# Two-layer hybrid trunk on one core: elementwise work of GpSimd moved to VectorE, norm sums and gate results in pieces, six raw buffers

## Chip, core and metric

The kernel runs on one core of a Trainium2 chip. The metric is the device time of one execution in microseconds (us). A profiled execution gives a trace: every instruction of TensorE (PE, its weight loads PEld), VectorE (DVE), ScalarE (ACT), GpSimd (POOL) and the DMA queue of SyncE (SP), with its start, its duration and what it waited for.

## What is computed

Batch 1, 256 tokens, width 2048, two layers, all in float32. Layer 0 has a Mamba-2 mixer (SSD), layer 1 forgetting attention (FoX). Cut to the frame:

```python
for i in range(DEPTH):
    hn = rmsnorm(h, norm_mix_pre[i])
    mix = ssd_mixer(hn, ...) if i % 2 == 0 else fox_mixer(hn, ...)
    h = h + rmsnorm(mix, norm_mix_post[i])
    ff = swiglu(rmsnorm(h, norm_ffn_pre[i]), ffn_w_gate[i], ffn_w_up[i], ffn_w_down[i])
    h = h + rmsnorm(ff, norm_ffn_post[i])
    pe = rmsnorm(p[i] @ ple_w_proj[i], ple_norm[i])
    h = h + jax.nn.sigmoid(h @ ple_w_gate[i]) * pe
```

rmsnorm divides by the root of the mean square over the 2048 features and multiplies by a weight. The last line of a layer is the per-layer input (PLE below).

## The kernel before

**Tiles.** h is kept transposed as 16 chunks `h[c]` of 128 features x 256 tokens. All weights (515 MB) stream from HBM once. A matmul input is split in two parts that together hold the float32: for activations `x[:, 0]` and `x[:, 1]` (`split`), for weights `wh` (a cast on ScalarE, L174) and `wl` (raw - wh on VectorE, L176). Each pair of weight tile and chunk gives TensorE a matmul of 512 columns (wh, L233) and one of 256 (wl, L235).

**Stages and units.** A unit is a product for 2 to 6 tiles of 128 outputs over all K chunks. It is cut into stages of at most 1024 weight columns: one chunk for a six-tile unit, two for a four-tile one, four for the two-tile one. A stage loads `raw` over SyncE's queue, casts wh and subtracts wl; raw, wh and wl have four buffers each. `next_stage` issues a stage two ahead (LOOK). After a unit the sums of its accumulators leave PSUM through `gather` (a copy on ScalarE, an add on VectorE). Six accumulator banks are shared by the units.

**Background.** `bg` is a list of small tasks; `unit` takes one after each stage. `drain` runs what is left. A scheduler with a timeline model of its own then orders the instructions of each engine; `tc.issue_after` holds an instruction behind another.

**An update.** After the mixer and after the FFN, `post_norm` forms 1/rms of the result (sums of squares in `ssb`, a matmul with ones, a power on GpSimd L287, a diagonal `dg` and one more matmul into `rwide`). The first unit that follows carries `mk_update`: for chunk c it adds the normed part `ts[c]` to h (L422 on VectorE; from c = 3 on every second chunk on GpSimd, L424), forms the next `ts` (L414), splits h into the next unit's input (L265 with a weight, L262 without), and, ahead of the FFN, squares h on ScalarE and adds the square to `ssb` on GpSimd (L274). Update A stands in the first gate unit of the FFN, update B in the first gate unit of PLE; there is one of each in each layer. The six-tile unit needs one chunk each stage.

**The FFN's first gate unit** also has `mk_r` at its end, which turns `ssb` into `rwide` and half of it, `rwide2`; then `ev_g` gathers each tile and forms silu (L487, a tanh on ScalarE, L490, L491), with the sums of squares of `pp` (`ssp`) as background of the up unit.

**PLE.** `pp` is p @ W_proj, `ssp` its sum of squares; `mkpe` forms `rpe`, `mkpp` scales pp on GpSimd (L537). Four units of 6, 4, 4 and 2 tiles compute the gate. `e3` closes a tile at the unit's end: tanh on ScalarE, L555 (tanh + 1 times pp), L556 (times weight, added to h), in layer 0 also the split for the attention (L265 into xb) and the square with its sum on GpSimd; in layer 1 it stores the chunk.

**V.** The attention of layer 1 starts with five units for V, with tokens as output rows: matmuls of 412 columns, wl of 824, eight stages each. At the end of the first stands the 1/rms of h.

**Start.** `prep0` splits each chunk of x as it arrives and adds its square to `ssb` on GpSimd; the first unit has five tiles and one chunk a stage.

## Time and profile before

| | before |
|---|---|
| median of 3 runs | 2798.67 us (2798.58 to 2799.8) |
| profiled execution | 2800.33 us |
| its span (first to last instruction) | 2798.5 us |
| TensorE's clock as granted, mean | 0.999 |

The busy time of an engine is the sum of its instructions; of two that overlap in the engine's pipeline the overlap counts once. A row of the timeline gives start and duration, engine, source line, operation, output<-inputs and the shape, and in brackets the idle time before it and what ended it. In a table of windows the columns are the window, its length, busy time and instructions of each engine asked for (TensorE alone, or TensorE, its weight loads, VectorE, ScalarE, GpSimd), then the granted clock as a share of full speed, the share of the DMA engines' time and GB/s. A row of waits gives what waited, for what, us in total, how often, and the longest.

### The profile page before, as it was taken

What the parts mean: (1) busy time and instruction counts of PE and PEld (TensorE: products, weight loads), DVE (VectorE), ACT (ScalarE), POOL (GpSimd) and SP (SyncE); (2) the same over time, 40 slices, a digit from 0 to 9 for tenths busy, and PEclk for the clock granted to TensorE, in tenths of its full rate; (3) what the DMA queues carried; (4) which work ended last, traced back from release to release, by engine and by line L of the source; (5) the groups of instructions that cost most, each with busy time, mean ns of one, the idle gap of its engine ahead of it and who ended that gap; (6) DMA issues with size and microseconds to landing.
All of it is one profiled execution on the core that took longest, in us unless ns stands there. A gap on an engine that the chain in (4) does not pass through costs nothing.

```text
span 2798.5 us, 43191 instructions
## 1 busy us (share of the span) xinstructions
PE 2768.2 (99%) x16306; PEld 2447.5 (87%) x16306; DVE 1926.0 (69%) x3033; ACT 1484.8 (53%) x2455; POOL 183.5 (7%) x236
## 2 busy tenths in 40 slices
PE   9999999999999999999999999999999999999999
PEld 8888888889788888888897998888888888888888
DVE  8888888855966645666669656766866545666577
ACT  6587676644654444444446544555654444445454
POOL 2000000000300000000005000000200000000022
PEclk9999999999999999999999999999999999999999
DMA  7666665565566656666555676655666556656545
GB/s 235 189 197 183 194 191 177 158 202 180 161 201 189 192 191 188 188 180 194 194 168 167 189 207 191 178 161 166 181 189 192 192 190 187 195 172 204 192 153 176
DMA packets 262512, 520.09 MB, mean 186 GB/s; under 512 B 17392, under 2 KB 42128, under 8 KB 262304
## 3 DMA queue, kind: packets, MB, share of 16 engines
q1 hardware_dynamic: 258640, 504.96, 58.8%
q0 software_dynamic: 3520, 12.15, 1.5%
q8 instruction: 127, 2.08, 0.3%
q14 instruction: 81, 0.66, 0.1%
q10 hardware_dynamic: 144, 0.24, 0.0%
HBM read 515.10 MB, written 2.18 MB: 185 GB/s over the span
## 4 chain that ended last, share of the span: by engine, by line
PE 91%; DVE 4%; issue 4%; ACT 1%; POOL 0%; DMA 0%; DVEq 0%; ACTq 0%; POOLq 0%
PE acc L233 53%; PE acc L235 28%; PE acc L230 1%; PE acc L229 1%; PE acc L228 1%; PE acc L223 1%; PE acc L222 1%; PE acc L224 1%; PE mi L751 1%; DVE x L265 1%; DVE wl L176 1%; DVE sg L414 1%; DVE x L262 0%; DVE h L422 0%; PE mi L753 0%
## 5 line engine op out<-in xcount | busy, mean ns | idle before, releaser
L233 PE MATMUL acc<-x,wh 128*128 128x512 f32 x5008 | 1718.9, 394 | 13.7 <-DVE x L265 6.6
L176 DVE TENSOR_TENSOR wl<-raw,wh 128x1024 fp32r<-128x1024 f32 (+4 forms) x1020 | 1183.2, 1166 | 782.4 <-ACT wh L174 778.8
L174 ACT CAST wh<-raw 128x1024 fp32r<-128x1024 f32 (+4 forms) x1020 | 1006.6, 993 | 989.0 <-PE acc L233 809.9
L235 PE MATMUL acc<-x,wl 128*128 128x256 f32 x5008 | 1340.0, 283 | 7.5 <-DVE wl L176 7.5
L233 PEld LDWEIGHTS acc<-x,wh 128*128 128x128 f32 x5008 | 928.2, 188 | 209.5 <-DVE x L265 14.7
L235 PEld LDWEIGHTS acc<-x,wl 128*128 128x128 f32 x5008 | 932.5, 189 | 33.1 <-DVE wl L176 10.9
L233 PE MATMUL acc<-a,wh 128*128 128x512 f32 x1232 | 425.5, 391 | 0.0
L235 PE MATMUL acc<-a,wl 128*128 128x256 f32 x1232 | 341.9, 282 | 0.0
L233 PEld LDWEIGHTS acc<-a,wh 128*128 128x128 f32 x1232 | 229.9, 188 | 47.1
L235 PEld LDWEIGHTS acc<-a,wl 128*128 128x128 f32 x1232 | 232.6, 189 | 2.2
L233 PE MATMUL acc<-xb,wh 128*128 128x512 f32 x512 | 181.9, 396 | 0.0
L256 ACT COPY tb<-acc 128x256 f32<-128x256 f32 (+1 forms) x401 | 139.6, 369 | 38.6 <-PE acc L235 19.0
L235 PE MATMUL acc<-xb,wl 128*128 128x256 f32 x512 | 145.8, 285 | 0.0
L287 POOL TENSOR_TENSOR rs<-ms,mhalf 128x2 f32<-128x2 f32 x18 | 21.2, 1177 | 1752.8 <-DVE ms L284 1752.8
L233 PEld LDWEIGHTS acc<-xb,wh 128*128 128x128 f32 x512 | 95.9, 188 | 19.3
L235 PEld LDWEIGHTS acc<-xb,wl 128*128 128x128 f32 x512 | 96.7, 189 | 0.7 <-issue 0.2
L257 DVE TENSOR_TENSOR g<-acc,tb 128x256 f32<-128x256 f32 x204 | 78.7, 415 | 2.1 <-ACT tb L256 1.6
L233 PE MATMUL acc<-xq,wh 128*128 128x512 f32 x224 | 77.6, 390 | 0.0
L733 ACT ACTIVATE E<-ab,bias 128x128 f32<-128x128 f32 x192 | 59.8, 390 | 15.3 <-PE mi L753 14.7
L661 DVE SCALAR_TENSOR_TENSOR g<-xr,vec,g 128x256 f32<-128x256 f32 x144 | 62.4, 476 | 4.0 <-ACT g L658 3.5
L235 PE MATMUL acc<-xq,wl 128*128 128x256 f32 x224 | 62.8, 282 | 0.0
L274 POOL TENSOR_TENSOR ssb<-ssb,sqp 128x256 f32<-128x256 f32 x60 | 55.5, 925 | 61.2 <-ACT sqp L273 56.7
(210 smaller groups left out, 2302.9 us busy)
## 6 DMA issues: line engine op xcount, KB each, us to landing
raw<-down SPq DMA_DIRECT2D x176, 512.0 KB, 4.1
raw<-ssd_in SPq DMA_DIRECT2D x152, 512.0 KB, 4.6
raw<-gate SPq DMA_DIRECT2D x128, 512.0 KB, 3.9
raw<-up SPq DMA_DIRECT2D x128, 512.0 KB, 4.5
raw<-fox_in SPq DMA_DIRECT2D x64, 512.0 KB, 3.9
raw<-gate SPq DMA_DIRECT2D x64, 384.0 KB, 3.4
raw<-up SPq DMA_DIRECT2D x64, 384.0 KB, 3.6
raw<-ssd_out SPq DMA_DIRECT2D x40, 512.0 KB, 3.7
```

The source lines that it names most:

```text
L174: A.copy(out=wh[:, :kc * n], in_=raw[:, :kc * n])
L176: V.tensor_tensor(out=wl[:, :kc * n], in0=raw[:, :kc * n], in1=wh.bitcast(F32)[:, :kc * n], op=sub)
L222: PE.matmul(o, lhsT=xh, rhs=wh[:, c, :], start=st, stop=False)
L223: PE.matmul(o, lhsT=xh, rhs=wl[:, c, :], start=False, stop=False)
L224: PE.matmul(o, lhsT=x[:, 1, t * P:(t + 1) * P], rhs=wh[:, c, :], start=False, stop=sp)
L233: PE.matmul(accs[t], lhsT=wh[:, c, t * P:(t + 1) * P], rhs=x.rearrange("p a n -> p (a n)"), start=st, stop=False)
L235: PE.matmul(accs[t][:, :T], lhsT=wl[:, c, t * P:(t + 1) * P], rhs=x[:, 0, :], start=False, stop=sp)
L256: A.copy(out=tb[:np_], in_=acc[:np_, T:2 * T])
L257: V.tensor_tensor(out=o, in0=acc[:np_, :T], in1=tb[:np_], op=add)
L274: (eng or V).tensor_tensor(out=acc, in0=acc, in1=sq, op=add)
L661: V.scalar_tensor_tensor(out=c, in0=xr[:, k:k + T], scalar=col(f"conv_w{k}", cc), in1=c, op0=mult, op1=add)
L733: A.activation(E[:, i, b * P:(b + 1) * P], ab[:, i, lo:lo + P], AF.Relu, scale=-1.0, bias=bias3[:, b, h0 + i:h0 + i + 1])
```

## The change

GpSimd keeps memsets, the power (L287) and its DMAs: its instructions go from 233 to 101 rows, VectorE's from 2978 to 3110. All h adds of an update are on VectorE. The squares of h after update A are summed in the up unit that follows (`late_norm`), as five pieces, each held behind the newest wl (`paced`); the wl after it is held behind the piece (`turn`). The silu of the first gate unit, which needs the 1/rms from those sums, moves into the up unit in four steps. In PLE a unit's end only gathers its tiles into ten `gz` buffers; `close` then does each tile in three parts, one stage apart, in the next unit, with the scaling of pp on VectorE. The sums for the first V unit run inside that unit, two tasks a stage. In an update, the next wh and wl are held behind the split of the chunk. raw has six buffers instead of four, which a smaller scratch for DMA descriptors makes room for.

The diff, cut to its core:

```diff
-RAWB = 4
+RAWB = 6
+SCRATCH = 8192
...
-H_POOL_EVERY = 2
...
-SSQ_AT = 4
...
+    low, turn, turn_a = [None], [], [None]
...
+        if a_ins is None:
+            a_ins, turn_a[0] = turn_a[0], None
...
+        with ExitStack() as order:
+            for ins in [v_ins] + turn:
+                order.enter_context(after(ins))
+            turn.clear()
+            low[0] = V.tensor_tensor(out=wl[:, :kc * n], in0=raw[:, :kc * n],
+                                     in1=wh.bitcast(F32)[:, :kc * n], op=sub)
...
-    def sumsq(acc, src, first, eng=None):
+    def sumsq(acc, src, first):
...
-            sq = tmp("sq" if eng is None else "sqp")
+            sq = tmp("sq", bufs=4)
...
-            (eng or V).tensor_tensor(out=acc, in0=acc, in1=sq, op=add)
+            last_v[0] = V.tensor_tensor(out=acc, in0=acc, in1=sq, op=add)
...
+    def sums_of(acc, src, cs, by=(2,) * 8):
+        cs = list(cs)
+        return [lambda cc=[cs.pop(0) for _ in range(n)]: [paced(sumsq, acc, src[i], i == 0)
+                                                          for i in cc] for n in by]
+    def paced(f, *args):
+        with tc.issue_after(low[0].ins):
+            r = f(*args)
+        turn.append(last_v[0])
+        return r
...
-            e = G if H_POOL_EVERY and c >= 3 and c % H_POOL_EVERY == 0 else V
-            if e is V:
-                chain(lambda: V.tensor_tensor(out=h[c], in0=h[c], in1=ts[c], op=add))
-            else:
-                G.tensor_tensor(out=h[c], in0=h[c], in1=ts[c], op=add)
+            chain(lambda: V.tensor_tensor(out=h[c], in0=h[c], in1=ts[c], op=add))
...
-            am = mark[0]
-            if wpre is not None:
-                sumsq(ssb, h[c], c == 0, G)
+            turn.append(prev[0])
+            turn_a[0] = mark[0]
...
-                emit_stage(am, prev[0])
+                emit_stage(mark[0], prev[0])
...
+            def silu_a(sg):
+                last_v[0] = V.tensor_tensor(out=sg, in0=sg, in1=rwide2, op=mult)
+                th = tmp("th")
+                mark[0] = A.activation(th, sg, AF.Tanh)
+                return th
+            def silu_b(sg, th):
+                V.scalar_tensor_tensor(out=sg, in0=th, scalar=1.0, in1=sg, op0=add, op1=mult)
+                last_v[0] = V.tensor_tensor(out=sg, in0=sg, in1=rwide, op=mult)
...
-                if first[0]:
-                    bg.append(noop)
-                    for c in range(8):
-                        bg.append(lambda c=c: late_ssp(pp, c))
-                    first[0] = False
...
+                if not first[0]:
+                    silu_b(sg, silu_a(sg))
+            def late_norm():
+                f1, f2 = mk_r()
+                bg.extend(sums_of(ssb, h, range(NCH), (3, 3, 3, 4, 3)))
+                bg.extend((noop, f1, noop, noop, f2, noop, noop))
+                ths = {}
+                def step(j):
+                    if j:
+                        for k in (j - 2, j - 1):
+                            paced(silu_b, sgs[k], ths[k])
+                    if j < len(sgs):
+                        for k in (j, j + 1):
+                            ths[k] = paced(silu_a, sgs[k])
+                for j in range(0, len(sgs) + 2, 2):
+                    bg.append(lambda j=j: step(j))
...
-                    unit(lambda k: xs[k], ev_g, pre=up, late=mk_r() if first[0] else (),
-                         look=0 if first[0] else LOOK)
-                    def ev_u(t, acc, c0=c0, acts=acts):
+                    unit(lambda k: xs[k], ev_g, pre=up, look=0 if first[0] else LOOK)
+                    begun = first[0]
+                    first[0] = False
+                    if begun:
+                        late_norm()
+                    def ev_u(t, acc, c0=c0, acts=acts, begun=begun):
+                        if begun and t == 0:
+                            drain()
+                            bg.append(noop)
+                            for c in range(8):
+                                bg.append(lambda c=c: late_ssp(pp, c))
...
-        def mkpp(c):
-            G.tensor_tensor(out=pp[c], in0=pp[c], in1=rpe, op=mult)
-        def ssq2():
-            for c in range(8, NCH):
-                late_ssp(pp, c, G)
...
+        ths = {}
+        def close_a(c, src):
+            ths[c] = gz[c] if c in gz else tmp("th")
+            A.activation(ths[c], src, AF.Tanh, scale=0.5)
+            last_v[0] = V.tensor_tensor(out=pp[c], in0=pp[c], in1=rpe, op=mult)
+        def close_b(c):
...
-            V.scalar_tensor_tensor(out=pe, in0=th, scalar=1.0, in1=pe, op0=add, op1=mult)
-            V.scalar_tensor_tensor(out=h[c], in0=pe, scalar=col(f"ple{i}", c), in1=h[c], op0=mult,
-                                   op1=add)
+            V.scalar_tensor_tensor(out=pe, in0=ths[c], scalar=1.0, in1=pe, op0=add, op1=mult)
+            last_v[0] = V.scalar_tensor_tensor(
+                out=h[c], in0=pe, scalar=col(f"ple{i}", c), in1=h[c], op0=mult, op1=add)
...
-                split(h[c], next_xs[c], col("mix_pre1", c))
-                sumsq(ssb, h[c], c == 0, G)
+                A.activation(next_xs[c][:, 0, :], h[c], AF.Copy, scale=col("mix_pre1", c))
+        def close_c(c):
+            if next_xs is not None:
+                x = next_xs[c]
+                last_v[0] = V.scalar_tensor_tensor(
+                    out=x[:, 1, :], in0=h[c], scalar=col("mix_pre1", c),
+                    in1=x.bitcast(F32)[:, 0, :], op0=mult, op1=sub)
+        def close(c):
+            if 0 <= c - 2:
+                paced(close_c, c - 2)
+            if 0 <= c - 1 < c_sep:
+                paced(close_b, c - 1)
+            if c < c_sep:
+                paced(close_a, c, gz[c])
+        def e3(t, acc, c0):
+            c = c0 + t
+            gz[c] = pn.tile([P, T], F32, tag="gz", name=nm("gz"), bufs=10)
+            gather(acc, gz[c])
+        def e3_last(t, acc, c0):
+            drain()
+            close_a(c0 + t, acc[:, :T])
+            close_b(c0 + t)
+            close_c(c0 + t)
...
-                bg.extend([noop] * SSQ_AT + [ssq2] + [noop] * (13 - SSQ_AT) + [mkpe])
-                for c in range(6):
-                    bg.append(lambda c=c: mkpp(c))
...
-                unit(lambda k: xs2[k], lambda t, acc: (drain(), e3(t, acc, 0)), pre=up, look=0)
-                for c in range(6, NCH):
-                    bg.append(lambda c=c: mkpp(c))
+            unit(lambda k: xs2[k],
+                 lambda t, acc, c0=c0, last=last: (e3_last if last else e3)(t, acc, c0),
+                 pre=up, look=LOOK if u else 0, pops=2 if u in (1, 3) else 1,
+                 merge=TAIL_STAGES if last else 1, sep=last)
+            if u == 0:
+                bg.extend(sums_of(ssp, pp, range(8, NCH), (1, 1, 2, 1, 2, 1)))
+                bg.extend((noop, pe_small, noop, noop, pe_wide, noop, noop))
+            if u == len(OUT0) - 2:
+                flush = (c_sep, c_sep + 1)
...
-                unit(lambda k: xs2[k], lambda t, acc, c0=c0: e3(t, acc, c0),
-                     merge=TAIL_STAGES if u == 3 else 1, sep=u == 3)
+                flush = ()
+            if not last:
+                for c in range(c0, c0 + n):
+                    bg.append(lambda c=c: close(c))
+                    if c < 2:
+                        bg.append(noop)
+                for c in flush:
+                    bg.append(lambda c=c: close(c))
...
-        sumsq(ssb, h[c], c == 0, G)
+        sumsq(ssb, h[c], c == 0)
...
+    v1, v2 = mk_r(False, rsm)
+    bg.extend(sums_of(ssb, h, range(NCH)))
...
-        unit(lambda k: nxt[k], ev_v(u), tok=True, late=mk_r(False, rsm) if u == 0 else ())
+        unit(lambda k: nxt[k], ev_v(u), tok=True, pops=2 if u == 0 else 1,
+             late=(lambda: (drain(), v1()), v2) if u == 0 else ())
...
-    nc = bacc.Bacc("TRN2", target_bir_lowering=False, num_devices=1)
+    nc = bacc.Bacc("TRN2", target_bir_lowering=False, num_devices=1,
+                   dynamic_dma_scratch_size=SCRATCH)
...
```

How VectorE's instructions stand is shown at three places (names with a buffer number behind; sg and pn are `ts`, m the mixer's result, vec the norm weights; the changed file has later line numbers). First update A in the first gate unit of layer 0, around chunks 4 to 6 (h_87 to h_89). Before:

```order
L414 SCALAR_TENSOR_TENSOR sg_7854<-m_4_6587,vec,rwide 128x256
L176 TENSOR_TENSOR wl_7902<-raw_7899,wh_7901 128x768
L265 SCALAR_TENSOR_TENSOR x_7671<-h_86,vec,x_7671 128x256
L414 SCALAR_TENSOR_TENSOR sg_7880<-m_5_6588,vec,rwide 128x256
L265 SCALAR_TENSOR_TENSOR x_7672<-h_87,vec,x_7672 128x256
L422 TENSOR_TENSOR h_88<-h_88,sg_7880 128x256
L414 SCALAR_TENSOR_TENSOR sg_7906<-m_6_6589,vec,rwide 128x256
L176 TENSOR_TENSOR wl_7928<-raw_7925,wh_7927 128x768
L265 SCALAR_TENSOR_TENSOR x_7673<-h_88,vec,x_7673 128x256
L414 SCALAR_TENSOR_TENSOR sg_7932<-m_7_6590,vec,rwide 128x256
L176 TENSOR_TENSOR wl_7954<-raw_7951,wh_7953 128x768
```

After the change:

```order
L436 TENSOR_TENSOR h_87<-h_87,sg_7847 128x256
L430 SCALAR_TENSOR_TENSOR sg_7870<-m_5_6588,vec,rwide 128x256
L181 TENSOR_TENSOR wl_7866<-raw_7863,wh_7865 128x768
L270 SCALAR_TENSOR_TENSOR x_7672<-h_87,vec,x_7672 128x256
L436 TENSOR_TENSOR h_88<-h_88,sg_7870 128x256
L430 SCALAR_TENSOR_TENSOR sg_7893<-m_6_6589,vec,rwide 128x256
L181 TENSOR_TENSOR wl_7889<-raw_7886,wh_7888 128x768
L270 SCALAR_TENSOR_TENSOR x_7673<-h_88,vec,x_7673 128x256
L436 TENSOR_TENSOR h_89<-h_89,sg_7893 128x256
L430 SCALAR_TENSOR_TENSOR sg_7916<-m_7_6590,vec,rwide 128x256
L181 TENSOR_TENSOR wl_7912<-raw_7909,wh_7911 128x768
```

Every chunk has its add on VectorE (L436) and one wl; before, only h_86, h_88 and so on were added there, and wl stood unevenly.

The second place is behind the first up unit of layer 0, where the second gate unit begins; g is a gathered up tile, a the product with the silu, acc the accumulators. Before, from the fourth wl of that unit to the fifth:

```order
L176 TENSOR_TENSOR wl_8675<-raw_8672,wh_8674 128x1024
L257 TENSOR_TENSOR g_839_8625<-acc_8291,tb_8626 128x256
L262 TENSOR_TENSOR a_7779<-g_837_8618,a_7779 128x256
L506 TENSOR_TENSOR g_839_8625<-g_839_8625,sg_8261 128x256
L257 TENSOR_TENSOR g_841_8632<-acc_8292,tb_8633 128x256
L506 TENSOR_TENSOR g_841_8632<-g_841_8632,sg_8270 128x256
L262 TENSOR_TENSOR a_7780<-g_839_8625,a_7780 128x256
L257 TENSOR_TENSOR g_843_8639<-acc_8293,tb_8640 128x256
L262 TENSOR_TENSOR a_7781<-g_841_8632,a_7781 128x256
L506 TENSOR_TENSOR g_843_8639<-g_843_8639,sg_8279 128x256
L262 TENSOR_TENSOR a_7782<-g_843_8639,a_7782 128x256
L176 TENSOR_TENSOR wl_8697<-raw_8694,wh_8696 128x1024
```

After the change, from the fourth wl on:

```order
L181 TENSOR_TENSOR wl_8653<-raw_8650,wh_8652 128x1024
L267 TENSOR_TENSOR a_7777<-g_826_8582,a_7777 128x256
L267 TENSOR_TENSOR a_7778<-g_828_8589,a_7778 128x256
L262 TENSOR_TENSOR g_830_8596<-acc_8199,tb_8597 128x256
L262 TENSOR_TENSOR g_832_8603<-acc_8200,tb_8604 128x256
L543 TENSOR_TENSOR g_830_8596<-g_830_8596,sg_8181 128x256
L543 TENSOR_TENSOR g_832_8603<-g_832_8603,sg_8185 128x256
L267 TENSOR_TENSOR a_7779<-g_830_8596,a_7779 128x256
L267 TENSOR_TENSOR a_7780<-g_832_8603,a_7780 128x256
L262 TENSOR_TENSOR g_834_8610<-acc_8201,tb_8611 128x256
L262 TENSOR_TENSOR g_836_8617<-acc_8202,tb_8618 128x256
L543 TENSOR_TENSOR g_834_8610<-g_834_8610,sg_8189 128x256
```

Four more rows of this kind and a sum of pp's squares follow there before the fifth wl, 15 rows in all between the two.

The third is the change from the last PLE unit (tiles 14 and 15 of pp, xb the attention's input) to V's first unit, whose wl have 824 columns. Before, from the second wl to the fifth:

```order
L176 TENSOR_TENSOR wl_16127<-raw_16124,wh_16126 128x824
L265 SCALAR_TENSOR_TENSOR xb_14990<-h_95,vec,xb_14990 128x256
L265 SCALAR_TENSOR_TENSOR xb_14991<-h_96,vec,xb_14991 128x256
L555 SCALAR_TENSOR_TENSOR pp_14_6613<-th_16178,pp_14_6613 128x256
L556 SCALAR_TENSOR_TENSOR h_97<-pp_14_6613,vec,h_97 128x256
L176 TENSOR_TENSOR wl_16217<-raw_16214,wh_16216 128x824
L265 SCALAR_TENSOR_TENSOR xb_14992<-h_97,vec,xb_14992 128x256
L176 TENSOR_TENSOR wl_16235<-raw_16232,wh_16234 128x824
L555 SCALAR_TENSOR_TENSOR pp_15_6614<-th_16187,pp_15_6614 128x256
L556 SCALAR_TENSOR_TENSOR h_98<-pp_15_6614,vec,h_98 128x256
L176 TENSOR_TENSOR wl_16253<-raw_16250,wh_16252 128x824
```

After the change, the last rows ahead of the third wl; the first and the second stand directly behind each other, with two closing rows between them and the first one shown here:

```order
L589 SCALAR_TENSOR_TENSOR h_97<-pp_14_6613,vec,h_97 128x256
L588 SCALAR_TENSOR_TENSOR pp_15_6614<-th_16129,pp_15_6614 128x256
L599 SCALAR_TENSOR_TENSOR xb_14989<-h_94,vec,xb_14989 128x256
L589 SCALAR_TENSOR_TENSOR h_95<-pp_12_6611,vec,h_95 128x256
L588 SCALAR_TENSOR_TENSOR pp_13_6612<-gz_15961,pp_13_6612 128x256
L589 SCALAR_TENSOR_TENSOR h_98<-pp_15_6614,vec,h_98 128x256
L599 SCALAR_TENSOR_TENSOR xb_14992<-h_97,vec,xb_14992 128x256
L589 SCALAR_TENSOR_TENSOR h_96<-pp_13_6612,vec,h_96 128x256
L599 SCALAR_TENSOR_TENSOR xb_14990<-h_95,vec,xb_14990 128x256
L599 SCALAR_TENSOR_TENSOR xb_14993<-h_98,vec,xb_14993 128x256
L599 SCALAR_TENSOR_TENSOR xb_14991<-h_96,vec,xb_14991 128x256
L181 TENSOR_TENSOR wl_16157<-raw_16154,wh_16156 128x824
```

The closings of tiles 10 to 15 stood among the wl before; now those that are left come in one row between the second wl and the third, and the sums (L279) follow between the next ones. L588 of pp_14, which needs the last unit's first tile, stands three rows ahead of the first wl.

More of the change, by code (lines that the diff above doesn't have):

```diff
@@ L172, in emit_stage @@
         wl = wp.tile([P, SW], F32R, tag="wl", name=f"wl{i}", bufs=WB)
+        if a_ins is None:
+            a_ins, turn_a[0] = turn_a[0], None
         with after(a_ins):
             A.copy(out=wh[:, :kc * n], in_=raw[:, :kc * n])
-        with after(v_ins):
-            V.tensor_tensor(out=wl[:, :kc * n], in0=raw[:, :kc * n],
-                            in1=wh.bitcast(F32)[:, :kc * n], op=sub)
+        with ExitStack() as order:
[4 more added lines that the diff above has]
+                                     in1=wh.bitcast(F32)[:, :kc * n], op=sub)
         emitted.append((view(wh), view(wl), kc))
@@ L244, in unit @@
             evac(t, accs[t])
-    mark, dmark = [None], [None]
+    mark, dmark, last_v = [None], [None], [None]
     def tmp(tag, shape=(P, T), dt=F32, bufs=2):
@@ L395, in post_norm, with late_ssp @@
             f()
-    def late_ssp(pp, c, eng=None):
+    def late_ssp(pp, c):
         with tc.issue_after(mark[0].ins):
-            sumsq(ssp, pp[c], c == 0, eng)
+            sumsq(ssp, pp[c], c == 0)
     def mk_update(new, m, wpost, wpre, xs):
@@ L529, in tail, with pe_small, pe_wide @@
         post_norm(filler(pp, (2, 3)))
[L531 to L533 removed]
+        def pe_small():
+            r_pe.append(rstd_small(ssp, D))
+        def pe_wide():
+            rstd_wide(r_pe[0], rpe)
             V.tensor_scalar(out=rpe, in0=rpe, scalar1=0.5, scalar2=None, op0=mult)
[L536 to L553 removed]
+        r_pe = []
+        gz = {}
+        c_sep = NCH - OUT0[-1]
+        ths = {}
[4 more added lines that the diff above has]
+        def close_b(c):
             pe = pp[c]
[L555 to L557 removed]
+            V.scalar_tensor_tensor(out=pe, in0=ths[c], scalar=1.0, in1=pe, op0=add, op1=mult)
+            last_v[0] = V.scalar_tensor_tensor(
+                out=h[c], in0=pe, scalar=col(f"ple{i}", c), in1=h[c], op0=mult, op1=add)
             if next_xs is None:
```

21 lines of the change are left out of this document (3 added, 18 removed).

## The prediction

> **What bounds the kernel now.** First the busy times, the cast's row and the chain of the page, then TensorE's waits: over the span, then in 1510 to 1530 us, in 2750 to 2768 and in 0 to 30.
>
> ```profile
> PE 2768.2 (99%) x16306; PEld 2447.5 (87%) x16306; DVE 1926.0 (69%) x3033; ACT 1484.8 (53%) x2455; POOL 183.5 (7%) x236
> L174 ACT CAST wh<-raw 128x1024 fp32r<-128x1024 f32 (+4 forms) x1020 | 1006.6, 993 | 989.0 <-PE acc L233 809.9
> PE 91%; DVE 4%; issue 4%; ACT 1%; POOL 0%; DMA 0%; DVEq 0%; ACTq 0%; POOLq 0%
> PE acc L233 <- DVE x L265: 6.6, 11, 1.5
> PE acc L233 <- DVE x L262: 3.7, 8, 0.8
> ...
> PE acc L235 <- DVE wl L176: 3.5, 2, 1.8
> ...
> PE acc L235 <- DVE wl L176: 1.6, 2, 1.2
> ...
> PE acc L235 <- DVE wl L176: 1.9, 2, 1.8
> ```
>
> TensorE is the bound (91% of the chain). The change removes no matmul, so all that it can win is time in which TensorE stands for VectorE, or runs at half clock after it stood. Those places are few. The casts on ScalarE idle 989 us, 810 of it until TensorE frees a weight buffer: loads are not the limit.
>
> What TensorE loses at an update is read from stage starts. The first two rows are chunk 0 and chunk 14 of the first gate unit of layer 0 (update A); the next two are chunk 0 and chunk 11 of the first gate unit of the per-layer input (update B); then TensorE alone in a later stretch.
>
> ```profile
> 706.15 0.50 PE L233 MATMUL acc<-x,wh 128*128 128x512 f32 x1
> 741.46 0.50 PE L233 MATMUL acc<-x,wh 128*128 128x512 f32 x1 [0.34 <-DVE x L265]
> 1455.22 0.50 PE L233 MATMUL acc<-x,wh 128*128 128x512 f32 x1
> 1481.46 0.50 PE L233 MATMUL acc<-x,wh 128*128 128x512 f32 x1
> 1485.00:1514.00 29.00, 29.00 (x169) 1.00 0.59 196
> ```
>
> Undisturbed, 169 matmuls take 29.00 us, 0.172 each: a stage of 12 (six tiles, one chunk) takes 2.06, one of 16 takes 2.75. Update A: 35.31 - 14 x 2.06 = **6.5 us lost**. Update B: 26.24 - 11 x 2.06 = **3.6 us lost**. Each comes once per layer.
>
> Why VectorE is late there is seen in its timeline in update A, with GpSimd's rows of the same time behind it.
>
> ```profile
> 718.01 0.96 DVE L265 SCALAR_TENSOR_TENSOR x<-h,vec,x 128x256 fp32r<-128x256 f32 x1
> 718.89 0.95 DVE L414 SCALAR_TENSOR_TENSOR sg<-m,vec,rwide 128x256 f32<-128x256 f32 x1
> 719.77 1.49 DVE L176 TENSOR_TENSOR wl<-raw,wh 128x768 fp32r<-128x768 f32 x1
> 721.18 0.47 DVE L265 SCALAR_TENSOR_TENSOR x<-h,vec,x 128x256 fp32r<-128x256 f32 x1
> 721.58 0.41 DVE L422 TENSOR_TENSOR h<-h,sg 128x256 f32<-128x256 f32 x1
> 721.91 0.47 DVE L414 SCALAR_TENSOR_TENSOR sg<-m,vec,rwide 128x256 f32<-128x256 f32 x1
> 722.31 0.94 DVE L176 TENSOR_TENSOR wl<-raw,wh 128x768 fp32r<-128x768 f32 x1
> 723.18 0.95 DVE L265 SCALAR_TENSOR_TENSOR x<-h,vec,x 128x256 fp32r<-128x256 f32 x1
> 717.30 1.38 POOL L424 TENSOR_TENSOR h<-h,sg 128x256 f32<-128x256 f32 x1 [1.10 <-DVE sg L414]
> 718.65 1.79 POOL L274 TENSOR_TENSOR ssb<-ssb,sqp 128x256 f32<-128x256 f32 x2
> ```
>
> While GpSimd adds (717.30 to 720.44) each VectorE instruction takes 0.95 or 1.49; when it rests (721.18 to 723.18) the same kinds take 0.41, 0.47 and 0.94. The four rows from 721.18 are one whole chunk without GpSimd: **2.00 us by their starts, under TensorE's 2.06**. The Trainium skill ("SBUF — State Buffer", section "SBUF: two separate sides") says that the two engines share a pair of ports under an exclusive lock, which an instruction holds from start to end; the 0.95 beside 0.47 agrees.
>
> **What moves, by kind.** Grouped by form: GpSimd's add of h against VectorE's, GpSimd's and VectorE's sum, and the scaling of pp that is on GpSimd now.
>
> ```profile
> L424 POOL TENSOR_TENSOR h<-h,sg 128x256 f32<-128x256 f32 x12 | 16.6, 1387 | 18.7 <-DVE sg L414 18.7
> L422 DVE TENSOR_TENSOR h<-h,sg 128x256 f32<-128x256 f32 x20 | 8.3, 413 | 0.1
> L274 POOL TENSOR_TENSOR ssb<-ssb,sqp 128x256 f32<-128x256 f32 x60 | 55.5, 925 | 61.2 <-ACT sqp L273 56.7 <-DVE wl L176 2.1
> L274 DVE TENSOR_TENSOR ssb<-ssb,sq 128x256 f32<-128x256 f32 x60 | 25.2, 421 | 10.6 <-ACT sq L273 8.8
> L537 POOL TENSOR_TENSOR pp<-pp,rpe 128x256 f32<-128x256 f32 x32 | 31.6, 1025 | 12.4 <-DVE rpe L534 12.4
> ```
>
> A moved instruction takes 0.41 to 0.42 on VectorE, 0.33 by starts (721.58 to 721.91). The 24 h adds, 76 sums and 32 scalings come to 132 x 0.33 = 44 us on an engine with 800 us idle; what counts is where they stand.
>
> **Update A.** This is the window over most of its chunks.
>
> ```profile
> 712.00:742.00 30.00, 27.81 (x147) 22.50 (x148) 30.00 (x43) 17.33 (x35) 18.15 (x18) 1.00 0.51 138
> ```
>
> VectorE is busy all 30 us, GpSimd 18 of them. Without GpSimd a chunk costs VectorE 2.00 us against 2.06, so I expect all 6.5 us gone. Given back: (1) At the end of the first gate unit the gathers stand behind one wl and a sum (0.87 + 0.33), and the up unit needs the banks that they free; less the 0.6 by which a wl is ahead, 0.6. (2) Sixteen sums and the silu run in the up unit.
>
> ```profile
> 744.00:778.00 34.00, 34.00 (x199) 29.91 (x198) 27.26 (x54) 20.25 (x39) 0.70 (x1) 1.00 0.72 214
> ```
>
> Before, that stretch leaves VectorE 6.7 us of 34 free; 15 sums of 0.33 are 5, and the silu work was in it already: it fits, with 0.35 for one crowded stage. (3) Behind the up unit's end 15 rows stand between the fourth and the fifth wl, where before ten did. Start 0.6 after the unit's end (a gather's copy), ten rows at 0.35, two wl at 1.13 (1.21 below, less the 0.08 by which the next starts ahead of an end, as at 721.58), fifteen rows, a wl: 12.8 us, against 4 stages x 2.75 = 11.0. That is 1.8; I take 1.3, as some of the silu rows may be done early. Net 6.5 - 2.3 = **4.2 per layer, 8.4** (4 to 13).
>
> **Update B.** One chunk is an add, a scaled product, a split and a wl, again 2.0 us: 3.6 gone. Given back at the unit's end, where a wl of 1024 (1.13) and a sum stand ahead of the gathers, less some slack: 1.1. Net **2.5 per layer, 5.0** (2.4 to 7.2).
>
> **Per-layer input.** First two wl of VectorE, one beside GpSimd's eleven scalings (third row) and one after them; then the half clock that follows, and V's start.
>
> ```profile
> 1515.51 1.75 DVE L176 TENSOR_TENSOR wl<-raw,wh 128x1024 fp32r<-128x1024 f32 x1
> 1523.44 1.21 DVE L176 TENSOR_TENSOR wl<-raw,wh 128x1024 fp32r<-128x1024 f32 x1
> 1504.81 11.37 POOL L537 TENSOR_TENSOR pp<-pp,rpe 128x256 f32<-128x256 f32 x11
> 1521.58:1524.99 3.41, 3.41 (x14) 2.89 (x13) 3.41 (x7) 2.91 (x8) 3.30 (x2) 0.50 0.59 194
> 1554.00:1572.00 18.00, 18.00 (x101) 17.98 (x100) 12.22 (x19) 8.64 (x13) 3.11 (x5) 1.00 0.67 194
> 1558.82 1.01 DVE L176 TENSOR_TENSOR wl<-raw,wh 128x824 fp32r<-128x824 f32 x1
> 1559.75 0.48 DVE L265 SCALAR_TENSOR_TENSOR xb<-h,vec,xb 128x256 fp32r<-128x256 f32 x1
> ```
>
> Layer 0 loses 3.5 us in two waits on wl and 1.7 at half clock (3.41 us at 0.50); layer 1 loses 1.6. In the changed order a stage has one wl (1.13) and one closing (two instructions at 0.34, two at 0.40): 2.61 of 2.75. It just fits, so 5.2 + 1.6 = **6.8** goes (3 to 6.8).
>
> **V's start** (layer 0 only) is where the change gives back. Before, the window from 1554 to 1572 holds no wait, though its wl lie among as many closings. Now V's first wl stands behind an instruction that needs the tanh of the last gate unit's first tile, which ends 10 matmuls (1.2 us) before the unit does. From the unit's end (estimates from rows): tanh at -0.65, three rows (1.1), a wl of 824 (0.93 by starts): 1.5 us late. The second wl ends at 2.4; then 13 rows (4 x 0.34 + 9 x 0.40 = 5.0) and the third, at 8.3. TensorE, resumed at 1.5, does two stages of 12 x 0.187 (18.00 us / 101 with a few records missing; estimate 4.5) and wants it at 6.0: 2.2 more. Waits 3.7; a wait of 1.8 at 1521 brought half clock, so I add 1.7: **-5.4** (-8 to 0). The Trainium skill ("TensorE: Matmul & The Clock Gate", section "Why this matters for your kernels") warns only of gaps over some 3 us. By it V's start would cost 3.7 alone; the half clock at 1521.58, which no gap that long precedes, speaks against it.
>
> **Start.** The first rows are VectorE's and GpSimd's beside each other, the last is the half clock behind the wait.
>
> ```profile
> 18.81 3.13 DVE L265 SCALAR_TENSOR_TENSOR x<-h,vec,x 128x256 fp32r<-128x256 f32 x4
> 16.02 3.46 POOL L274 TENSOR_TENSOR ssb<-ssb,sqp 128x256 f32<-128x256 f32 x3 [0.32 <-ACT sqp L273]
> 23.10:26.50 3.40, 3.40 (x14) 2.92 (x13) 3.40 (x6) 1.89 (x4) 1.14 (x2) 0.50 0.56 163
> ```
>
> TensorE waits 1.8 for a wl behind the four splits at 18.81, then runs at half clock for 3.4 us (1.7). In the new order no four splits stand together, two of the raw loads are issued earlier, and a chunk costs 0.40 + 0.33 + 0.73 (a wl of 640, by 0.87 x 640 / 768, an estimate) = 1.46 of its 1.72 (10 matmuls). 3.5 could go; I take **2.5** (0 to 3.5), since the h loads set the pace too. Six raw buffers get nothing of their own: the casts wait for TensorE. The pins (wl after a chunk's split) cost nothing where VectorE keeps 2.00 under 2.06; without that cover each would cost its stage's lag.
>
> **Sum.** 8.4 + 5.0 + 6.8 - 5.4 + 2.5 = 17.3. The profiled execution took 2800.33 us (span 2798.5), so 2783.0 on that footing; the median 2798.67 is 1.7 lower and close to the span, and gives 2781.4: **2782 us**.
>
> **Rivals.**
> (1) *Nothing is given back*: the closings and gathers find slack, V starts without a wait. For it: VectorE is 69% busy. Against: rows counted at V's start. All losses gone: 13 + 7.2 + 6.8 + 3.5 = 30.5, so 2768; from 2774 down I count as this case. Chance 0.12.
> (2) *Waits only change place*: gains at the updates come back at unit boundaries, where gathers and silu queue behind wl, and V costs 8. By the low ends: 4 + 2.4 + 3 - 8 = 1.4, so 2797. For it: the closings use 2.61 of 2.75. Chance 0.13, a third of that still over 0.2% faster.
> (3) *Slower, by pinned pieces*: a sum waits for its square on ScalarE, and the next wl waits for the sum. VectorE's sums now lose 0.15 us each to that (8.8 us over 60). Pinned pieces are about 70 (10 steps of sums in the up units, 8 of silu, 12 of ssp, 32 closings, 8 in V). If ScalarE's square stands behind a cast that waits for a buffer, each delays its wl; above 0.25 us a piece (17.3 / 70) the gain is gone, at 0.4 the kernel is 11 us slower: 2809. For it: a stage at 2.61 of 2.75 has no room. Against: casts are two stages ahead. Chance 0.07.
> (4) *V's waits bring no half clock*: a wait of 1.5 us in update A brought none (the granted clock of 712 to 742 is 1.00), so 1.5 and 2.2 may not either. Then 2782 - 1.7 = 2780. Chance 0.2, taken out of the forecast's case and inside its bounds. The Trainium skill's page "TensorE: Matmul & The Clock Gate" would give this one.
> (5) *VectorE is slow for another reason*, and GpSimd's absence does not speed it. Against it, the rows from 721.18. Under 0.02, counted in (3).
>
> My forecast (2774 to 2793) keeps 0.48, with rival 4 0.68. What this kernel's measurement tells from no change is about 0.2%, 5.6 us: faster is under 2793. Faster 0.68 + 0.12 + 0.04 = 0.84, same 0.09, slower 0.07. Range 2771 to 2796: above lie rival 3 and half of the same cases, below a part of rival 1.
>
> **What would show it.** After: x L265 and sg L414 at 0.47 in update A and no wl above 1.25; starts of chunks 0 and 14 under 29.5 us apart; no half clock near the per-layer input of layer 0; waits of 1.5 and 2 us with half clock at V's start. Wrong if VectorE's instructions stay at 0.95 with GpSimd idle, or if TensorE's waits on wl grow in the units behind the updates.

## The result and the profile after

| | before | changed |
|---|---|---|
| median | 2798.87 us (4 runs, 2798.58 to 2799.8) | 2781.64 us (4 runs, 2781.18 to 2783.61) |
| span of the profiled execution | 2798.5 us | 2779.8 us |
| ratio | | 0.9939, 95% interval 0.9922 to 0.9956 |

The kernel is 0.6% faster, 17.2 us; 2782 was predicted. The page of the changed kernel, its busy times and its chain:

```profile
PE 2758.7 (99%) x16306; PEld 2446.8 (88%) x16306; DVE 1909.7 (69%) x3165; ACT 1482.3 (53%) x2455; POOL 50.8 (2%) x104
PE 97%; DVE 2%; ACT 1%; issue 0%; DMA 0%; POOL 0%; SPq 0%; DVEq 0%; ACTq 0%; POOLq 0%
```

VectorE took 132 instructions from GpSimd and is busy for 16 us less than before: what it took on cost less than what GpSimd's company had cost. TensorE's waits (for what, us in all, times, longest):

```profile
PE acc L228 <- DVE wl L181: 4.0, 2, 2.5
PE mi L312 <- DVE dg L309: 3.5, 4, 0.9
PE acc L238 <- DVE gz L262: 1.8, 2, 0.9
PE acc L240 <- DVE wl L181: 1.7, 3, 0.6
...
PE acc L238 <- DVE sg L262: 0.9, 2, 0.4
```

The waits on the updates' splits (6.6 us, of which 0.8 at the start, and 3.7 us before) are gone. New are V's start (first row), the gathers behind the first gate units (gz and sg), and a wl in the gate unit behind the first up unit (in the fourth row, 0.6 us in each layer). Update A in layer 0, by VectorE's timeline, and chunks 0 and 14 on TensorE:

```profile
708.33 0.48 DVE L270 SCALAR_TENSOR_TENSOR x<-h,vec,x 128x256 fp32r<-128x256 f32 x1
708.72 0.42 DVE L436 TENSOR_TENSOR h<-h,sg 128x256 f32<-128x256 f32 x1
709.06 0.48 DVE L430 SCALAR_TENSOR_TENSOR sg<-m,vec,rwide 128x256 f32<-128x256 f32 x1
709.46 0.95 DVE L181 TENSOR_TENSOR wl<-raw,wh 128x768 fp32r<-128x768 f32 x1
710.32 0.48 DVE L270 SCALAR_TENSOR_TENSOR x<-h,vec,x 128x256 fp32r<-128x256 f32 x1
...
701.47 0.50 PE L238 MATMUL acc<-x,wh 128*128 128x512 f32 x1
730.70 0.39 PE L238 MATMUL acc<-x,wh 128*128 128x512 f32 x1
```

A chunk costs VectorE 1.99 us, and the fourteen stages take 29.23 us in place of 35.31.

Laid over each other matmul by matmul, the two traces show where the changed kernel's lead grows and where it shrinks. Numbers are the lead gained in that part, in us, read to some 0.2.

| part | predicted | measured |
|---|---|---|
| start | 2.5 | 4.7 |
| update A, layer 0: gain, given back | 6.5, -2.3 | 6.4, -2.0 |
| update B, layer 0 | 3.6, -1.1 | 3.4, -1.5 |
| per-layer input, layer 0 | 5.2 | 5.8 |
| V's start | -5.4 | -6.2 |
| update A, layer 1 | 6.5, -2.3 | 6.1, -1.9 |
| update B, layer 1 | 3.6, -1.1 | 3.3, -1.2 |
| per-layer input, layer 1 | 1.6 | 2.1 |
| sum | 17.3 | 19.0 (18.7 by the spans) |

### The profile page after: what moved, and what is told of

The parts are those of the page before. It is cut to its first block, busy times and chain, and to the rows that moved or that the text cites. A ratio compares the mean times of both kernels' runs of the same rounds, so it can differ in the third digit from the quotient of the medians.

```text
span 2779.8 us, 43097 instructions
## 1 busy us (share of the span) xinstructions
PE 2758.7 (99%) x16306; PEld 2446.8 (88%) x16306; DVE 1909.7 (69%) x3165; ACT 1482.3 (53%) x2455; POOL 50.8 (2%) x104
## 4 chain that ended last, share of the span: by engine, by line
PE 97%; DVE 2%; ACT 1%; issue 0%; DMA 0%; POOL 0%; SPq 0%; DVEq 0%; ACTq 0%; POOLq 0%
PE acc L238 56%; PE acc L240 30%; PE acc L234 1%; PE acc L233 1%; PE acc L235 1%; PE acc L228 1%; PE acc L229 1%; PE acc L227 1%; PE mi L820 1%; DVE wl L181 1%; ACT wh L176 0%; PE mi L822 0%; PE mi L312 0%; PE mi L296 0%; PE mi L787 0%
## 5 line engine op out<-in xcount | busy, mean ns | idle before, releaser
L262 DVE TENSOR_TENSOR g<-acc,tb 128x256 f32<-128x256 f32 x176 | 67.2, 417 | 0.3
L228 PE MATMUL acc<-wl,xb 128*128 128x412 f32 (+1 forms) x160 | 56.8, 355 | 4.0 <-DVE wl L181 4.0
```

The costliest lines, as they stand in the source:

```text
L228: PE.matmul(o, lhsT=xh, rhs=wl[:, c, :], start=False, stop=False)
L262: V.tensor_tensor(out=o, in0=acc[:np_, :T], in1=tb[:np_], op=add)
```

## Experiments

All times are medians, compared with the changed kernel's 2781.64 us and with runs of the kernel before on the same chip in the same session (medians 2798.87 to 2799.26). The changed kernel was timed in a session of its own, so a difference from it of less than a microsecond is not read. "By the lead" means that two traces are laid over each other as in the table, one execution of each. In code lines a sign ahead of a line marks the edit against the kernel named.

### One part undone: every second h add on GpSimd again

```diff
-            chain(lambda: V.tensor_tensor(out=h[c], in0=h[c], in1=ts[c], op=add))
+            if c >= 3 and c % 2 == 0:
+                G.tensor_tensor(out=h[c], in0=h[c], in1=ts[c], op=add)
+            else:
+                chain(lambda: V.tensor_tensor(out=h[c], in0=h[c], in1=ts[c], op=add))
```

> One part undone: from chunk 3 on every second h add of an update is on GpSimd again, the sums and closings stay as changed. My theory (VectorE is slowed by whatever elementwise instruction runs beside it on GpSimd): a GpSimd add of 1.39 us makes two or three VectorE instructions take 0.95 in place of 0.45, so two chunks cost VectorE about 4.0 - 0.33 + 1.1 = 4.8 us against TensorE's 4.12; six such pairs in each of four updates, some 2.5 to 3.5 us an update: 2790 to 2796. Rival (the gain is that the sums were taken out of the updates; the adds' engine doesn't matter): within 2 us of 2781.6.

Measured: **2777.03 us** (2776.69 to 2777.33), 4.6 us *faster* than the changed kernel. My theory's number was wrong by 13 us, and the rival (within 2 us of 2781.6) missed it too. VectorE and GpSimd in update A of this run:

```profile
708.92 0.47 DVE L270 SCALAR_TENSOR_TENSOR x<-h,vec,x 128x256 fp32r<-128x256 f32 x1
...
710.04 0.95 DVE L181 TENSOR_TENSOR wl<-raw,wh 128x768 fp32r<-128x768 f32 x1
710.91 0.96 DVE L270 SCALAR_TENSOR_TENSOR x<-h,vec,x 128x256 fp32r<-128x256 f32 x1
711.80 0.48 DVE L430 SCALAR_TENSOR_TENSOR sg<-m,vec,rwide 128x256 f32<-128x256 f32 x1
...
713.06 0.48 DVE L270 SCALAR_TENSOR_TENSOR x<-h,vec,x 128x256 fp32r<-128x256 f32 x1
710.20 1.39 POOL L437 TENSOR_TENSOR h<-h,sg 128x256 f32<-128x256 f32 x1 [2.75 <-DVE sg L430]
```

GpSimd's add lasts 1.39 us, but only one VectorE instruction is slowed, by 0.49 (0.96 - 0.47). The wl that ran when the add began is not slowed (0.95). Read as a turn-taking, the add waits out the wl that is running (some 0.7 us of its 1.39), then the next VectorE instruction waits for the add. So **an add on GpSimd costs VectorE 0.49 us and saves it 0.33**; two chunks take 4.14 us (708.92 to 713.06) where TensorE needs 4.12. The adds never were the cost once the sums had left. I had counted by how long GpSimd runs, not by how many instructions it runs.

Why it is faster shows at the ends of the units. Lead over the changed kernel is won in three places: 1.2 us behind update B in each layer, 1.3 at V's start. The first, in the changed kernel and then in this run:

```profile
1478.66 1.23 DVE L181 TENSOR_TENSOR wl<-raw,wh 128x1024 fp32r<-128x1024 f32 x1 [0.85 <-ACT wh L176]
1479.80 0.42 DVE L279 TENSOR_TENSOR ssp<-ssp,sq 128x256 f32<-128x256 f32 x1
1480.14 0.75 DVE L262 TENSOR_TENSOR gz<-acc,tb 128x256 f32<-128x256 f32 x2
```

```profile
1475.69 2.58 DVE L181 TENSOR_TENSOR wl<-raw,wh 128x1024 fp32r<-128x1024 f32 x2 [0.23 <-ACT wh L176]
1478.42 1.34 DVE L262 TENSOR_TENSOR gz<-acc,tb 128x256 f32<-128x256 f32 x3
```

With the adds away the scheduler placed the gathers ahead of the sum and of the third wl. That is a by-product of another order, not a merit of the adds on GpSimd.

### GpSimd made busy for nothing

```diff
+            for _ in range(2):
+                G.tensor_tensor(out=tmp("sq", bufs=4), in0=h[c], in1=h[c], op=add)
```

> The changed kernel, with two adds per chunk on GpSimd during each update that read h and write a tile that nobody reads: no work or wait of the kernel depends on them. My theory: some 0.9 us each, 1.8 of each chunk's 2.06 us; VectorE's chunk goes from 2.0 to 2.4 us or more, update A loses 5 to 8 us and update B 3 to 6 again, in both layers: 2797 to 2808. Rival (GpSimd was only late with results that others needed, and takes nothing from VectorE by running): 2781 to 2783.

The two lines stand in each update, behind the split of each chunk.

Measured: **2824.02 us** (2823.86 to 2824.41), 42 us slower than without them, more than expected. Nobody reads what GpSimd writes there. Update A, VectorE and GpSimd, and TensorE's waits for gathers:

```profile
715.00 0.47 DVE L430 SCALAR_TENSOR_TENSOR sg<-m,vec,rwide 128x256 f32<-128x256 f32 x1
715.39 1.36 DVE L181 TENSOR_TENSOR wl<-raw,wh 128x768 fp32r<-128x768 f32 x1
716.68 0.83 DVE L270 SCALAR_TENSOR_TENSOR x<-h,vec,x 128x256 fp32r<-128x256 f32 x1
717.43 0.41 DVE L436 TENSOR_TENSOR h<-h,sg 128x256 f32<-128x256 f32 x1
717.77 0.47 DVE L430 SCALAR_TENSOR_TENSOR sg<-m,vec,rwide 128x256 f32<-128x256 f32 x1
...
715.22 2.01 POOL L443 TENSOR_TENSOR sq<-h 128x256 f32<-128x256 f32 x2 [0.76 <-DVE h L436]
...
PE acc L238 <- DVE gz L262: 4.7, 2, 2.4
...
PE acc L238 <- DVE sg L262: 3.1, 2, 1.5
```

A chunk is 2.77 us instead of 1.99: each of the two instructions costs VectorE 0.39. This shows that GpSimd takes time from VectorE by running these adds, with no result involved. By the lead each of the four updates loses 9.2 us, thirteen chunks at (2.77 - 2.06), where I had allowed 8 for update A and 6 for update B: 37 us in all. Another 6 came behind the updates, where gathers were late by up to 2.4 and 1.5 us.

### The same with memsets

```diff
+            dm = tmp("sq", bufs=4)
+            G.tensor_tensor(out=dm[:, :2], in0=h[c][:, :2], in1=h[c][:, :2], op=add)
+            for _ in range(4):
+                G.memset(dm, 0.0)
```

> As the run with idle adds, but GpSimd's instructions per chunk are an add of 128x2 that reads h and four memsets of 128x256, which read nothing. If GpSimd slows VectorE only while it reads its operands: 2781 to 2784, and VectorE's instructions in update A stay at 0.41 to 0.47. If it slows VectorE by running at all: as far above as the memsets are long, over 2786 if a chunk's four take over a microsecond.

Measured: **2780.79 us** (2780.43 to 2781.41), the changed kernel's time. VectorE and GpSimd:

```profile
709.42 0.95 DVE L181 TENSOR_TENSOR wl<-raw,wh 128x768 fp32r<-128x768 f32 x1
710.29 0.47 DVE L270 SCALAR_TENSOR_TENSOR x<-h,vec,x 128x256 fp32r<-128x256 f32 x1
710.69 0.42 DVE L436 TENSOR_TENSOR h<-h,sg 128x256 f32<-128x256 f32 x1
...
709.87 0.55 POOL L443 TENSOR_TENSOR sq<-h 128x2 f32<-128x2 f32 x1
710.48 1.42 POOL L445 MEMSET sq<- 128x256 f32 x4
```

GpSimd is busy all the time (0.55 + 1.42 of each 1.99 us) and VectorE runs at 0.42, 0.47 and 0.95. The memsets, which read nothing, take nothing. The section of the Trainium skill that the prediction names ("SBUF — State Buffer", section "SBUF: two separate sides") limits the lock against a VectorE instruction with two SBUF inputs to GpSimd instructions that read SBUF; these two runs agree with it.

### The sums and adds on VectorE, but where they stood

The kernel before, with this edit and no more:

```diff
-H_POOL_EVERY = 2
+H_POOL_EVERY = 0
...
-            (eng or V).tensor_tensor(out=acc, in0=acc, in1=sq, op=add)
+            V.tensor_tensor(out=acc, in0=acc, in1=sq, op=add)
```

> The kernel before, with the h adds and all sums on VectorE at the places where they stood (the scaling of pp stays on GpSimd, no pieces, no pins). If GpSimd's company were the whole cost, this would win nearly what the change wins at the updates: 2783 to 2787. By the price that the run with the adds back shows (a GpSimd instruction delays VectorE by 0.49 us, on VectorE it takes 0.33): a chunk of update A costs 2.00 + 0.33 = 2.33 against TensorE's 2.06, and A still loses 3.8 of its 6.5 us; update B gains 2 to 3 us, the per-layer input nothing: 2788 to 2793.

Measured: **2794.72 us** (2792.94 to 2796.11), ratio to before 0.9984 (0.9975 to 0.9993): a quarter of the gain. That is 1.7 us above the bounds by the price, and 8 above the case in which GpSimd's company is the whole cost. The start wins 4.3 us of lead by 30 us, 3.4 from 42 us on. The fourteen stages of update A take 33.45 us, where they took 35.31 before and take 29.23 in the changed kernel. VectorE's timeline there:

```profile
709.99 0.47 DVE L265 SCALAR_TENSOR_TENSOR x<-h,vec,x 128x256 fp32r<-128x256 f32 x1
710.39 0.41 DVE L422 TENSOR_TENSOR h<-h,sg 128x256 f32<-128x256 f32 x1
710.73 0.47 DVE L414 SCALAR_TENSOR_TENSOR sg<-m,vec,rwide 128x256 f32<-128x256 f32 x1
711.12 0.41 DVE L274 TENSOR_TENSOR ssb<-ssb,sqp 128x256 f32<-128x256 f32 x1
711.46 0.94 DVE L176 TENSOR_TENSOR wl<-raw,wh 128x768 fp32r<-128x768 f32 x1
712.33 0.47 DVE L265 SCALAR_TENSOR_TENSOR x<-h,vec,x 128x256 fp32r<-128x256 f32 x1
```

No instruction is slowed and VectorE has no gap, but a chunk takes it 2.34 us, as worked out, and TensorE needs 2.06. Update B gains 0.3 us. The per-layer input loses 2.1 us in layer 0 and 0.7 in layer 1; in layer 0 one wait replaces two, and TensorE runs at half clock around its end for 6.8 us (the row's 0.50):

```profile
PE acc L235 <- DVE wl L176: 3.4, 1, 3.4
...
1503.18:1510.00 6.82, 5.77 (x18) 5.00 (x19) 6.82 (x10) 3.01 (x6) 0.00 (x0) 0.50 0.58 184
```

So taking the sums from GpSimd is not enough; they have to leave the update.

### The adds alone on VectorE

The kernel before with `H_POOL_EVERY = 0` alone.

> The kernel before with the h adds alone moved to VectorE; its sums stay on GpSimd inside the updates. By the price of 0.49 us for a GpSimd instruction against 0.33 on VectorE: update A costs 2.00 + 0.49 = 2.49 us a chunk against 2.40 before, update B 2.0 plus the sums of ssp: 2796 to 2801. Rival (the adds on GpSimd, the longest of its instructions, were the cost): 2788 to 2793.

Measured: **2808.59 us** (2807.35 to 2808.99), ratio 1.0033 (1.0021 to 1.0045), **slower than before**, and over 7 us past my bound. The rival is out: the longest of GpSimd's instructions were not the cost. The excess is in update B, in VectorE's timeline:

```profile
1462.57 0.48 DVE L414 SCALAR_TENSOR_TENSOR pn<-m,vec,rwide 128x256 f32<-128x256 f32 x1
1463.61 0.96 DVE L176 TENSOR_TENSOR wl<-raw,wh 128x768 fp32r<-128x768 f32 x1 [0.57 <-ACT wh L174]
1464.48 0.42 DVE L262 TENSOR_TENSOR x<-h,x 128x256 fp32r<-128x256 f32 x1
...
1469.03 0.95 DVE L262 TENSOR_TENSOR x<-h,x 128x256 fp32r<-128x256 f32 x1
```

Before 1468.8 GpSimd does nothing here, yet VectorE idles 0.57 us on a wl whose cast is not there, with the split that TensorE needs behind it. From 1468.8 the sums of ssp make every instruction 0.95. The idling on a cast is a second mechanism, at a place where GpSimd is idle, and the next run tests it.

### Without the pins

```diff
-            turn.append(prev[0])
-            turn_a[0] = mark[0]
...
-        turn.append(last_v[0])
```

> The changed kernel without its pins: the next wl and wh are not held behind the chunk's split or behind the piece (sums, silu, closings) that went before; the pieces themselves still follow the newest wl. My theory (VectorE needs 2.00 us a chunk against 2.06, in whatever order): 2780 to 2785. Rival (without pins wl run ahead of the splits that TensorE needs first, and pieces bunch up): over 2787.

Measured: **2789.96 us** (2789.8 to 2791.19), 8.3 us slower; the rival was right. VectorE in update A:

```profile
708.87 0.48 DVE L429 SCALAR_TENSOR_TENSOR sg<-m,vec,rwide 128x256 f32<-128x256 f32 x1
709.86 0.96 DVE L181 TENSOR_TENSOR wl<-raw,wh 128x768 fp32r<-128x768 f32 x1 [0.52 <-ACT wh L176]
710.74 0.48 DVE L270 SCALAR_TENSOR_TENSOR x<-h,vec,x 128x256 fp32r<-128x256 f32 x1
```

It is the same picture. The order of VectorE's kinds has hardly changed, but a wl stands two stages further ahead and waits for a cast on ScalarE, and the split behind it is late. VectorE's sum of 1.99 us was never the whole condition. By the lead, each of the four updates loses 3.3 us and the unit behind the first up unit 0.8 in each layer, while V's start *wins* some 6, since there the pins hold wl behind closings.

### The pins of the updates alone

The changed kernel without the line `turn.append(last_v[0])` in `paced`.

> The changed kernel with the pins of the updates (the next wl behind the chunk's split) and without the pins behind pieces (sums, silu, closings). My theory after the run without any pins (the pins of the updates won its 10 us there; those behind pieces cost 4 at V's start, where wl must wait for closings): updates as in the changed kernel, V's start some 4 us better, up to 3 us lost again in the units with pieces: 2777 to 2781. Rival (the pins behind pieces carry the gain): over 2784.

Measured: **2776.76 us** (2776.7 to 2776.82), 4.9 us faster than the changed kernel and just under my range. The fourteen stages of update A take 29.24 us, as in the changed kernel, against 32.43 without any pins: the pins of the updates carry that gain, four times 3.3 us. Those behind pieces cost more than they bring: by the lead some 6 us at V's start against 0.8 in each layer behind the first up unit.

### Four raw buffers

```diff
-RAWB = 6
+RAWB = 4
```

> The changed kernel with four raw buffers in place of six (the smaller DMA scratch stays). My theory (the casts wait for TensorE, so loads further ahead win nothing): 2781 to 2783. Rival (the two further buffers feed the start, where the raw loads come late beside the loads of x): 2783 to 2786, with the loss in the first 30 us.

Measured: **2784.84 us** (2783.97 to 2785.2), 3.2 us slower, inside the rival's bounds. By the lead 2.3 us of it lie in the first 42 us. That rests on one execution of each, and the start of another run with the changed kernel's code there (the one with two winners together) was 1.5 us later. The ratios to before, 0.9948 (0.9934 to 0.9963) here and 0.9939 (0.9922 to 0.9956) for the changed kernel, overlap. So what the two buffers are worth is not shown.

### The last closings among V's wl

```diff
-            drain()
-            close_a(c0 + t, acc[:, :T])
-            close_b(c0 + t)
-            close_c(c0 + t)
+            c = c0 + t
+            if next_xs is None:
+                drain()
+                close_a(c, acc[:, :T])
+                close_b(c)
+                close_c(c)
+            else:
+                close_a(c, acc[:, :T])
+                bg.extend((lambda: paced(close_b, c), lambda: paced(close_c, c)))
...
-                 pre=up, look=LOOK if u else 0, pops=2 if u in (1, 3) else 1,
+                 pre=up, look=LOOK if u else 0, pops=2 if u == 1 or last and next_xs is None else 1,
...
-        drain()
+        if next_xs is None:
+            drain()
```

> The closings left at the end of the last gate unit of layer 0 are not drained ahead of V but taken as background between V's first wl (chunks 12 to 15 are needed only in V's seventh and eighth stage), and that gate unit takes one background task a stage. My theory (V's start loses 6.2 us, two waits of 1.5 and 2.5 and half clock, because thirteen closing instructions stand between V's second wl and its third): the waits and the half clock go, 2775 to 2778. Rival (VectorE's work in V's first unit, 18 us in 18, is the limit, and the wait only moves a few stages on): 2779 to 2782.

Measured: **2777.23 us** (2776.39 to 2778.36), 4.4 us faster than the changed kernel; the theory held. The window over V's start in this run and in the changed kernel (TensorE's busy time and matmuls first, the granted clock third from the end):

```profile
1537.00:1553.00 16.00, 15.76 (x87) 15.35 (x87) 14.56 (x31) 10.47 (x19) 0.59 (x1) 1.00 0.52 156
```

```profile
1537.00:1553.00 16.00, 12.02 (x58) 11.32 (x57) 14.99 (x33) 9.75 (x21) 0.58 (x1) 0.89 0.46 131
```

In the same 16 us TensorE starts 87 matmuls instead of 58, and the half clock is gone.

### Two winners together

The adds back on GpSimd and the closings among V's wl.

> Both earlier winners together: every second h add from chunk 3 on GpSimd, and the last closings of layer 0 among V's first wl. With the adds back V still lost one wait of 2.9 us and half clock behind it (some 4.6 us); if that goes as it did alone: 2772 to 2774. Rival (the two won the same microseconds, at the unit boundary of the per-layer input and at V): 2775 to 2777.

Measured: **2773.76 us** (2773.23 to 2774.66), ratio to before 0.9911 (0.9897 to 0.9926): 7.9 us under the changed kernel, 25 under the one before; no kernel measured here was faster. Of the two gains alone (4.6 and 4.4), 1 us was shared at V's start, where by the lead the adds back win 1.3 us alone and nothing beside the closings.

### The same with the pins of the updates alone

The last kernel without the line `turn.append(last_v[0])` in `paced`.

> Adds back on GpSimd, closings among V's wl, and pins in the updates only. The pins behind pieces cost 4.9 us in the changed kernel, most of it at V's start, which the closings among V's wl have cured already. My theory (the gain at V can be had once): 2772 to 2775. Rival (those pins cost elsewhere too): 2769 to 2771.

Measured: **2774.77 us** (2773.55 to 2775.99), not told apart from the 2773.76 of the run before. What the pins behind pieces cost was at V's start, and is won once.

## Why the prediction was right, and where its reasons were not

**The sum held term by term, but for the start.** Update A was to win 6.5 and give back 2.3 us: 6.4 and 2.0, 6.1 and 1.9. Update B 3.6 and 1.1: 3.4 and 1.5, 3.3 and 1.2. The per-layer input 5.2 and 1.6: 5.8 and 2.1. These came from starts of matmuls and rows of VectorE, and needed only that a chunk without GpSimd takes VectorE 2.00 us, whatever the reason. That the time came within 0.4 us of 2782 is partly luck. Between the two traces the lead is 18.7 us, 1.4 more than the sum: the start won 2.2 more than its term and the per-layer input 1.1 more, V's start lost 0.8 more. Between the medians it is 17.2, since the profiled execution of the kernel before (2800.33) lay 1.5 above its median.

**V's start** was worked out as two waits of 1.5 and 2.2 us and a half clock. The trace has them, and the clock behind the second:

```profile
1539.56 0.45 PE L228 MATMUL acc<-wl,xb 128*128 128x412 f32 x1 [1.49 <-DVE wl L181]
1546.83 0.45 PE L228 MATMUL acc<-wl,xb 128*128 128x412 f32 x1 [2.49 <-DVE wl L181]
...
1546.83:1551.40 4.57, 4.57 (x16) 4.43 (x17) 4.19 (x9) 2.79 (x7) 0.00 (x0) 0.63 0.59 150
```

4.57 us at 0.63 is 1.7 us lost, the price taken. Rival 4 (no half clock) is out, and with it the reading of the Trainium skill's warning ("TensorE: Matmul & The Clock Gate", section "Why this matters for your kernels") as a threshold: a wait of 2.5 us was enough. But the length of a wait alone doesn't decide it: in the run with idle adds a wait of 2.35 us (ending at 1501.56) came with half clock and one of 2.36 (at 2761.32) without. At the start of the kernel before, a wait of 1.76 us came with half clock; in the run with the adds alone, one of 1.87 at the same place came without.

**"Without GpSimd a chunk costs VectorE 2.00 us against 2.06, so I expect all 6.5 us gone"** is right for the changed kernel and incomplete as a reason. Two more conditions had to hold. The sums had to leave the update: on VectorE at their old places update A's fourteen stages keep 4.2 of the 6.1 us that the changed kernel takes from them (33.45 against 29.23). And the wl had to stay behind the splits: the prediction said that the pins "cost nothing" and priced their benefit at nothing, while they carry 8.3 us net (2789.96 without them), and those of the updates 13.2 (2789.96 to 2776.76).

**The price of a GpSimd instruction.** "While GpSimd adds (717.30 to 720.44) each VectorE instruction takes 0.95 or 1.49" was read as slowness that lasts as long as GpSimd runs. It is about 0.4 to 0.5 us for each GpSimd instruction that reads a tile of 128x256, recorded at 1.0 us in the run with idle adds and at 1.39 in the one with the adds back; an h add is then nearly as cheap there as on VectorE (0.49 against 0.33). That the adds had to move was the part of the change that won nothing (2777.03 with every second one back).

**"Six raw buffers get nothing of their own"** is in doubt: without the two further buffers the kernel was 3.2 us slower, but the place and the cause of that are not shown. The term of the start was too small, 2.5 predicted and 4.7 measured; 3.4 of it also came with four buffers, by the sums on VectorE alone (the inline run). The casts' idle time, summed over the span, pointed to TensorE; the start is 1% of the span and does not show in that sum.

Rival 1 (nothing given back) is out for this kernel, and rival 2 (waits only change place) is right in part: of 15.6 us won at the three places of layer 0, 2.0, 1.5 and 6.2 came back.

Rival 3 (pinned pieces hold up wl) named the wrong place. Sums that wait for their squares are no more of a loss than before: VectorE idles 8.3 us for squares ahead of its 120 sums into ssb, where it idled 8.8 ahead of 60. The pins behind pieces cost 4.9 us net, and that at V's start, where wl wait for closings. Rival 5 is out by the run with idle adds.

What stays open is how much of the loss of the run with the adds alone comes from wl that stand too far ahead: pinning them in that kernel was not tried. Nor was the gain in the per-layer input taken apart: no run has the closings spread over the next unit with the scaling of pp still on GpSimd, or the other way round.

## What to carry over

When an engine waits for another that is slowed by a third, count the third engine's instructions and what each costs the second, not the time for which it is busy; then ask which of them can leave the crowded stretch, since moving them within it may win nothing or lose. A sum over the span says nothing of a stretch of 1%: read such places by their own windows. Where an instruction is moved ahead for safety, look at what it waits for, because all that stands behind it on its engine waits too.

## What the runs showed of the hardware

A GpSimd instruction that reads 128x256 delays VectorE by 0.39 to 0.49 us; four memsets of the same tile (1.42 us) and an add of two columns delay it by nothing that shows. At V's start TensorE's clock fell to half behind a wait of 2.5 us (2.9 in the run with the adds back); the wait of 1.5 us in the stage before brought none. Elsewhere waits between 1.76 and 2.36 us came both with half clock and without. In the inline run the half clock around a wait of 3.4 us lasted 6.8 us, twice the 3.41 us in the kernel before.
